# A decoder layer with a streamed cache: the pace of the stream, its rest before a pool switch, and norm factors in two parts

## The chip, the cores and the metric

The kernel runs on one core of a Trainium2 chip. The time is that of the device for one execution of the program, in microseconds (us), on that core. Lower is better. Engines are called as in the profile: PE (TensorE, matrix products), DVE (VectorE), ACT (ScalarE), POOL (GpSimd), SP (SyncE, which only issues DMAs).

## The reference

One step of a hybrid decoder layer for 512 prompt tokens and 32 sample tokens (8 sequences of 4), in float32. Cut to what matters here:

```python
z = rms_norm(x) @ w_in                      # (tokens, 2560): q, k, v, u, gv
q = rms_norm(q per head half of 64); k = rms_norm(k per head half of 64)
gv = rms_norm(gelu(gv) per group of 128); u = gelu(u)
att = softmax(q0 k0) v - lam * softmax(q1 k1) v        # prompt: causal, 512 tokens
att_s = the same for the 32 sample tokens, over 4096 cached keys and values
        of each of the 8 sequences (gathered by a page table) and the new ones
mix = u * (W_s gv + b)                      # within chunks of 128 positions
h   = x + [rms_norm(att), mix] @ w_out
out = h + relu(rms_norm(h) @ w_up)**2 @ w_down         # 1024 -> 4096 -> 1024
```

The cache holds 8 x 4096 rows of keys and as many of values, 512 floats each: 134 MB in all, which the kernel must read once.

## The kernel before

**The main program.** `in_proj` makes the input projection in ten pieces of 256 columns (q0 q1 k0 k1 v0 v1 g0 g1 u0 u1), each for four token tiles of 128 and the 32 sample rows; a piece's tiles come in two pairs (`tp` 0 and 1). Then come the prompt's attention (16 units), the output projection, and the feed-forward part (`ffn`) in eight groups of 512 hidden columns: in a group, an up product for each of the four tiles of 128 hidden columns (two passes `pr`, in each two tiles `f`, and each in two halves), then a down product with its own four parts. Float32 is made of a high and a low part, so a product is three matmuls: `wh` and `wl` are the parts of a weight tile `raw` (ACT casts the high part, DVE makes the low one), `Thi` and `Tlo` those of the tokens, `a_hi` and `a_lo` (both named `a`) those of the squared relu. `square` makes these: relu on ACT to `t`, the square on DVE, a cast on ACT, a difference on DVE. SP loads the weights, 512 KB each.

**The norm factors.** For q and k pieces `post` puts the sums of squares of each tile into a few columns of `ssb` (4 per tile, 2 in g pieces; DVE). When all tiles are there, `finish_piece` queues `stat`, which makes the factors of the whole piece on POOL with `rsqrt` (a short instruction that scales, then a long one that raises to the power -1/2), then `norm(i)` for each tile (DVE, or DVE and ACT, to `zn`) and `tr(i)` (PE transposes, `d<-idt,zn`). `later(fn, d)` queues a step and `flush`, called between pieces of the main program, runs what is due.

**The stream.** The cache of the 32 sample tokens is read in 64 chunks of 512 rows, 1 MB of keys and 1 MB of values each. POOL issues the gathers (`gK`, `gV`: DMA_INDIRECT to `kraw` and `v`; two `kraw`, four `v` buffers). For a chunk, `k_tr` transposes the keys on DVE to `kt` and then asks for the key load two chunks on; `scores` (PE, `S<-kt,qz`, two chunks at a time); after eight chunks (one sequence) `sm1` and `sm2` make the softmax (`s`, the matmul `d<-s,Rm`, the maximum `mc`, the exponentials `P` on ACT); `ptr` transposes on DVE and copies to `PT` on ACT (16 copies each); `av` multiplies with the values (PE, `O<-v,PT`) and then asks for the value load four chunks on; `fin1` scales (DVE `om`) and `fin2` sums with a matmul (`d<-om,selb`). The entries stand in the list `micro` in this order, each with a weight, 65.0 in all. Every `yield cost` of the main program goes to `pump`, which puts out as many entries as the credit pays for:

```python
    TAU = (122.7 + 44.8 * G1 + 30.0 * ATTW) / sum(w for w, _ in micro)   # G1 = 5, ATTW = 1.6
    def pump(dt):
        kv["t"] += dt
        while kv["i"] < len(micro) and kv["t"] >= micro[kv["i"]][0] * TAU:
            w, fs = micro[kv["i"]]
            kv["t"] -= w * TAU
            kv["i"] += 1
            for f, args in fs:
                f(*args)
```

The stream ends in feed-forward group 4 (`switch`), where the pools of the stream are closed ahead of the second pass:

```python
            if switch and pr == 1:
                while kv["i"] < len(micro):
                    pump(1.0)
                second_phase()
```

**The order.** A scheduler orders each engine's instructions. The wrapper `Ordered` (whose `call`, line 52, is the line of nearly all rows of the profile) binds it: POOL keeps the order of the program, PE and DVE may move an instruction past at most 28, and ACT's order is free. A tile's name says what is written, and what it is read from stands behind the arrow.

The functions that the diff touches and those that call them, with the line numbers of the profile:

Of the kernel before, what the change touches and what calls it, by code (L numbers as in the profile page):

```python
# [20 lines left out]
EPS = 1e-6  # L21
# [4 lines left out]
G1 = 5  # L26
# [9 lines left out]
ATTW = 1.6  # L36
# [26 lines left out]
def kernel(  # L63
# [230 lines left out]
    def later(fn, d=1):  # L294

        pend[d - 1].append(fn)
# [7 lines left out]
    def rsqrt(x, eps, mul=1.0):  # L304

        n, k = x.shape
        if eps or mul != 1.0:
            G.tensor_scalar(out=x, in0=x, scalar1=mul, scalar2=eps, op0=ALU.mult, op1=ALU.add)
        G.tensor_tensor(out=x, in0=x, in1=mhalf[:n, 0:k], op=ALU.pow)
# [74 lines left out]
    def pinned(on):  # L384

        for e in (V, A, PE, G, SP):
            e.window = 1 if on or e is G else WINDOW if e is V or e is PE else 0
# [282 lines left out]
    micro = []  # L670
# [26 lines left out]

    micro.append((0.2, [(lambda: sample_merge(), ())]))
    kv = {"i": 0, "t": 0.0, "on": False}
    TAU = (122.7 + 44.8 * G1 + 30.0 * ATTW) / sum(w for w, _ in micro)  # L700

    def pump(dt):

        if not kv["on"]:
            return
# [7 lines that stand above are left out]
# [45 lines left out]
        V.transpose(out=qT4[:, 8 * p:8 * p + 8, :], in_=zs[0:32].rearrange("p (f d) -> p f d", f=8))  # L758
        later(lambda: tr_pair(zs, 32, qTs[:, 2 * p:2 * p + 2, :], None), 2)

    def finish_piece(kind, p, ss, items):
        cols = slice(256 * p, 256 * p + 256)
        w = 4 if kind in "qk" else 2

        def stat():
            rsqrt(ss[:, 0:w * len(items)], EPS if kind in "qk" else 4.0 * EPS)

        def norm(i):
            z, n, t = items[i]
            sc = ss[:n, w * i:w * i + w]  # L770
            if kind == "g":
                gv_norm(z, n, sc, 2 * p)
                if t == 4:
                    SP.dma_start(out=gso[:, cols], in_=aux["gvs"][:, cols])
                return
            head_norm(z, n, sc, kg if kind == "k" else None)
            if kind == "k":
                SP.dma_start(out=kp[:, t, cols] if t < 4 else kso[:, cols], in_=z[:n])

        def tr(i):  # L780
            z, n, t = items[i]
            if kind == "g":
                return
            dst = (qT if kind == "q" else kT)[:, 2 * p:2 * p + 2, 128 * t:128 * t + 128] if t < 4 else \
                kTs[:, 2 * p:2 * p + 2, :]
            tr_pair(z, n, dst, qcol if kind == "q" else None)

        later(stat)
        for i in range(len(items)):
            later(lambda i=i: norm(i), 1 + i // 2)  # L790
            later(lambda i=i: tr(i), 3 + i // 2)

# [43 lines left out]
    def in_proj(gm, F, gsrc, junk):  # L836
        held = []
        pinned(True)
        zq = []

        def first_q(p):
            held.append((w_get(), w_get()))
            sps = dt_()[0:64, 0:256]
            for hf in range(2):
                packed(*held[p][hf], [(4 * hf + b, b) for b in range(4)], sps, hf == 0, hf == 1)
            return sps

        def first_stat(p, sps):
            z = combine(sps)
            zq.append(head_stat(z[0:32], 32, cst[0:32, 4 * p:4 * p + 4], 4))  # L850

        def first_keys():
            x_tile(2)
            k_tr(0)
            for p in range(2):
                q_sample(p, zq[p], cst[0:32, 4 * p:4 * p + 4])
            k_tr(1)
            kv["on"] = True

        sps = first_q(0)  # L860
        x_tile(0)
        w_conv()
        x_gain(gm, 1)
        x_stat(0, [xt[0]], 128, junk, G)
        x_gain(gm, 2)
        x_tile(1)
        x_gain(gm, 3)
        first_stat(0, sps)
        first_stat(1, first_q(1))
        rsqrt(cst[:32, 0:8], EPS)  # L870
        first_keys()
        yield 1.7
        att = attention()
        nt = new_tokens()
        for pi in range(10):
            kind, p = "qkvgu"[pi // 2], pi % 2
            if pi == 4:
                aux["vs"] = vgs
            if pi == 6:
                R3 = big.tile([128, 4 * T], F32, tag="r3", name="mix")  # L880
                R.append(R3)
                mix.append(R3[:, 0:2048].rearrange("p (n c) -> p n c", n=4))
                aux["gvs"] = vgs
            ss = ssb[pi % 2]
            items = []
            if kind == "q":
                A_, B_ = held[p]
            else:
                A_, B_ = w_get(), w_get()
            for tp in range(2):  # L890
                pss = {}
                if 2 * pi + tp == ATT0:
                    for _ in range(4):
                        flush()
                    local_pool(3)
                for half, w in ((0, A_), (1, B_)):
                    for t in (2 * tp, 2 * tp + 1):
                        cost = next(att, 0.0) if 2 * pi + tp >= ATT0 else 0.0
                        if half == 0:
                            pss[t] = dt_()[:, 0:256]  # L900
                        optB(pss[t], t, *w, half)
                        if t == 3 and (half == 0 or pi != 1):
                            w_conv()
                        if t % 2 == 1:
                            flush()
                        if half == 1:
                            post(kind, p, t, pss[t], 128, ss, items)
                            if pi == 4 and t == 0:
                                params()
                            if pi == 4 and t == 3:  # L910
                                params2()
                            if pi == 9 and t > 0:
                                cat_tile(t - 1)
                            if t == 3 and items:
                                finish_piece(kind, p, ss, items)
                            if pi == 0 and t == 1:
                                pinned(False)
                        elif pi == 5:
                            next(nt, None)
                        if pi == 0:  # L920
                            if t == 1 and half == 0:
                                x_stat(1, xt[1:4], 128, junk, G)
                                x_tile(3)
                            if t == 1 and half == 1:
                                masks(F, gsrc)
                            if t == 3 and half == 0:
                                gcols(gsrc)
                        if pi == 1 and t == 0 and half == 1:
                            load_params()
                        yield 1.3 + cost  # L930
                    if tp == 0 and kind != "q":
                        if half == 0:
                            sps = dt_()[0:64, 0:256]
                        packed(*w, [(4 * half + b, b) for b in range(4)], sps, half == 0, half == 1)
                        if half == 1:
                            post(kind, p, 4, combine(sps)[0:32], 32, ss, items)
                        yield 0.9
        yield from out_proj(att)

    def new_tokens():  # L940
# [212 lines left out]
    def ffn(start, joint, last, small, switch=False):  # L1153
        rng = [(0, 272), (272, 544)] if joint else [(0, 512)]
        n = T if joint else TP
# [14 lines left out]
        for pr in range(2):  # L1170
# [21 lines left out]
            for f in range(2):  # L1192
                if start and pr == 0:
                    square([psf[f]], f)
                    continue
                ps = [dt_() for _ in rng]
                for half in range(2):
                    hiw, low = hp[half]
                    for b in range(4):
                        k = 4 * half + b  # L1200
                        fc = slice(128 * f, 128 * f + 128)
                        for w, (st_w, mv) in enumerate(((hiw, Thi), (hiw, Tlo), (low, Thi))):
                            for q, (a, e) in enumerate(rng):
                                mm(ps[q][:, 0:e - a], st_w[:, b, fc], mv[:, k, a:e], k == 0 and w == 0, k == 7 and w == 2)
                    if f == 1:
                        w_conv()
                    if half == 0:
                        flush()
                        yield 2.8
                ff = 2 * pr + f  # L1210
                square(ps, ff)
                yield 2.8
# [237 lines left out]
```

## Time and profile before

| | |
|---|---|
| median of 3 runs | 822.18 us (821.0 to 822.18) |
| profiled execution | 821.3 us, of which the span from the first to the last instruction is 819.6 |
| mean granted clock of PE | 0.991 |
| busy: PE, weight loads, DVE, ACT, POOL | 97%, 77%, 66%, 44%, 22% |
| read from memory | 213.53 MB, 266 GB/s over the span |

Busy is the time in which an engine works on an instruction; the weight loads overlap PE's matmuls. In a row of a timeline, the time in brackets is the idle time ahead of the instruction, and behind the arrow stands what ended it.

### The profile page before, as it was taken

The numbers are of one execution on the slowest core, as the hardware profiler recorded it, in microseconds if no ns is written. First come the engines' busy times: TensorE is split into PE (matmuls) and PEld (weight loads), VectorE is DVE, ScalarE is ACT, GpSimd is POOL, SyncE is SP. The second block draws the span as 40 slices with busy tenths as digits, with TensorE's granted clock in tenths as the row PEclk, the third lists the DMA queues.
The fourth block names the chain that finished last, engine by engine and source line by source line (L and its number), as shares of the span: only waits on it lengthen the run. The fifth ranks groups of instructions, "written<-read, shape, count | busy, mean of one in ns | idle before, by whom it ended". The sixth has DMA issues, their size and how long they took to land.

```text
span 819.6 us, 15373 instructions
## 1 busy us (share of the span) xinstructions
PE 795.7 (97%) x6210; PEld 632.9 (77%) x6210; DVE 537.1 (66%) x883; ACT 358.6 (44%) x892; POOL 178.2 (22%) x196
## 2 busy tenths in 40 slices
PE   5899999999999999999999999998999999999997
PEld 4888887767667888867776777675676999998997
DVE  5878866898997856887677667653464534444254
ACT  4644743776585466463144235234243431331331
POOL 4553431344241222221322321213010000000000
PEclk9799999999999999999999999999999999999999
DMA  8597698787787888877997888877459677576202
GB/s 296 207 391 280 240 344 314 272 317 285 279 321 273 309 310 309 325 283 282 366 366 304 318 325 336 322 264 261 168 182 339 209 244 239 174 239 214 70 18 94
DMA packets 101798, 219.05 MB, mean 267 GB/s; under 512 B 6090, under 2 KB 83999, under 8 KB 85343
## 3 DMA queue, kind: packets, MB, share of 16 engines
q0 software_dynamic: 18432, 134.23, 42.4%
q1 hardware_dynamic: 83294, 83.84, 31.5%
q8 instruction: 49, 0.80, 0.4%
q14 instruction: 23, 0.18, 0.1%
HBM read 213.53 MB, written 4.52 MB: 266 GB/s over the span
## 4 chain that ended last, share of the span: by engine, by line
PE 73%; DVE 8%; issue 8%; ACT 4%; DMA 3%; POOL 2%; SPq 0%; DVEq 0%; POOLq 0%; ACTq 0%
PE d L52 64%; PE S L52 5%; PE O L52 5%; DVE kt L52 2%; ACT PT L52 2%; DMA kraw<-in_cache_k_dram,idxK 2%; DMA v<-in_cache_v_dram,idxK 1%; DMA raw<-in_w_in_dram 1%; ACT wh L52 1%; POOL v L52 1%; DVE zn L52 1%; DVE s L52 1%; POOL ssb L52 1%; DVE wl L52 1%; POOL kraw L52 1%
## 5 line engine op out<-in xcount | busy, mean ns | idle before, releaser
L52 ACT CAST wh<-raw 128x1024 fp32r<-128x1024 f32 x90 | 94.2, 1047 | 175.8 <-PE d L52 139.2
L52 PE MATMUL d<-a,wh 128*128 128x272 f32 (+1 forms) x704 | 168.3, 341 | 0.0
L52 DVE STREAM_TRANSPOSE kt<-kraw 128x2048 f32<-128x2048 f32 x64 | 146.3, 2297 | 16.6 <-PE S L52 7.4
L52 DVE TENSOR_TENSOR wl<-raw,wh 128x1024 fp32r<-128x1024 f32 x90 | 109.7, 1220 | 50.8 <-ACT wh L52 50.4
L52 PEld LDWEIGHTS d<-a,wh 128*128 128x128 f32 x704 | 113.2, 188 | 25.1 <-issue 6.3
L52 PE MATMUL d<-wh,Thi 128*128 128x256 f32 x432 | 127.7, 296 | 1.6 <-ACT t L52 1.6
L52 POOL DMA_INDIRECT v<-in_cache_v_dram,idxK x64 | 64.6, 1009 | 281.3 <-PE O L52 270.9
L52 PE MATMUL d<-wl,Thi 128*128 128x256 f32 x432 | 122.9, 285 | 0.0
L52 PE MATMUL d<-wh,Tlo 128*128 128x256 f32 x432 | 122.3, 284 | 0.0
L52 PE MATMUL d<-Thi,wh 128*128 128x272 f32 (+2 forms) x368 | 108.1, 334 | 0.0
L52 PE MATMUL d<-Tlo,wh 128*128 128x272 f32 (+2 forms) x368 | 106.5, 330 | 0.0
L52 PE MATMUL d<-Thi,wl 128*128 128x272 f32 (+2 forms) x368 | 106.4, 329 | 0.0
L52 PE MATMUL d<-a,wl 128*128 128x272 f32 (+1 forms) x352 | 104.2, 337 | 0.0
L52 PEld LDWEIGHTS d<-wh,Thi 128*128 128x128 f32 x432 | 82.3, 191 | 9.0 <-issue 4.8
L52 POOL DMA_INDIRECT kraw<-in_cache_k_dram,idxK x64 | 69.6, 1088 | 83.8 <-DVE kt L52 49.9
L52 PEld LDWEIGHTS d<-wh,Tlo 128*128 128x128 f32 x432 | 82.3, 191 | 0.4 <-issue 0.4
L52 PEld LDWEIGHTS d<-wl,Thi 128*128 128x128 f32 x432 | 82.1, 190 | 0.4 <-issue 0.4
L52 PEld LDWEIGHTS d<-Thi,wh 128*128 128x128 f32 x368 | 63.5, 188 | 15.6 <-issue 5.4
L52 ACT COPY PT<-d 32x128 f32<-32x128 f32 x256 | 65.6, 256 | 10.7 <-DVE d L52 7.5
L52 PEld LDWEIGHTS d<-Thi,wl 128*128 128x128 f32 x368 | 63.4, 188 | 6.2
L52 PEld LDWEIGHTS d<-Tlo,wh 128*128 128x128 f32 x368 | 63.7, 188 | 5.8
L52 PEld LDWEIGHTS d<-a,wl 128*128 128x128 f32 x352 | 60.5, 188 | 7.4 <-issue 0.4
(270 smaller groups left out, 1063.5 us busy)
## 6 DMA issues: line engine op xcount, KB each, us to landing
raw<-in_w_up_dram SPq DMA_DIRECT2D x32, 512.0 KB, 5.5
raw<-in_w_down_dram SPq DMA_DIRECT2D x32, 512.0 KB, 5.1
plain<-in_w_up_dram SPq DMA_DIRECT2D x20, 512.0 KB, 4.9
plain<-in_w_down_dram SPq DMA_DIRECT2D x20, 512.0 KB, 5.6
raw<-in_w_in_dram SPq DMA_DIRECT2D x18, 512.0 KB, 10.1
raw<-in_w_out_dram SPq DMA_DIRECT2D x8, 512.0 KB, 10.1
plain<-in_w_out_dram SPq DMA_DIRECT2D x8, 512.0 KB, 4.6
r<-in_x_prompt_dram SPq DMA_DIRECT2D x4, 512.0 KB, 9.0
```

The source lines that it names most:

```text
L52: r = f(*args, **kw)
```

## The change

Three edits. The constant of `TAU` falls from 122.7 to 117.7. In `ffn` of group 4, after the first half of the second up product of the first pass, the entries of the stream except the last five are put out. And the factors of a piece with norms are made in two parts: `early_stat` queues them for the first pair of tiles (and in k and g pieces the sample rows) when that pair is done, and `finish_piece` gets their number `n0`, makes the factors of the rest only, and queues this ahead of `norm(2)` and not ahead of `norm(0)`.

```diff
--- before.py
+++ after.py
@@ -697,7 +697,7 @@
 
     micro.append((0.2, [(lambda: sample_merge(), ())]))
     kv = {"i": 0, "t": 0.0, "on": False}
-    TAU = (122.7 + 44.8 * G1 + 30.0 * ATTW) / sum(w for w, _ in micro)
+    TAU = (117.7 + 44.8 * G1 + 30.0 * ATTW) / sum(w for w, _ in micro)
 
     def pump(dt):
 
@@ -758,12 +758,18 @@
         V.transpose(out=qT4[:, 8 * p:8 * p + 8, :], in_=zs[0:32].rearrange("p (f d) -> p f d", f=8))
         later(lambda: tr_pair(zs, 32, qTs[:, 2 * p:2 * p + 2, :], None), 2)
 
-    def finish_piece(kind, p, ss, items):
+    def early_stat(kind, ss, items):
+
+        n = (4 if kind in "qk" else 2) * len(items)
+        later(lambda: rsqrt(ss[:, 0:n], EPS if kind in "qk" else 4.0 * EPS))
+        return len(items)
+
+    def finish_piece(kind, p, ss, items, n0):
         cols = slice(256 * p, 256 * p + 256)
         w = 4 if kind in "qk" else 2
 
         def stat():
-            rsqrt(ss[:, 0:w * len(items)], EPS if kind in "qk" else 4.0 * EPS)
+            rsqrt(ss[:, w * n0:w * len(items)], EPS if kind in "qk" else 4.0 * EPS)
 
         def norm(i):
             z, n, t = items[i]
@@ -785,8 +791,9 @@
                 kTs[:, 2 * p:2 * p + 2, :]
             tr_pair(z, n, dst, qcol if kind == "q" else None)
 
-        later(stat)
         for i in range(len(items)):
+            if i == 2:
+                later(stat)
             later(lambda i=i: norm(i), 1 + i // 2)
             later(lambda i=i: tr(i), 3 + i // 2)
 
@@ -912,7 +919,7 @@
                             if pi == 9 and t > 0:
                                 cat_tile(t - 1)
                             if t == 3 and items:
-                                finish_piece(kind, p, ss, items)
+                                finish_piece(kind, p, ss, items, n0)
                             if pi == 0 and t == 1:
                                 pinned(False)
                         elif pi == 5:
@@ -935,6 +942,8 @@
                         if half == 1:
                             post(kind, p, 4, combine(sps)[0:32], 32, ss, items)
                         yield 0.9
+                if tp == 0 and items:
+                    n0 = early_stat(kind, ss, items)
         yield from out_proj(att)
 
     def new_tokens():
@@ -1207,6 +1216,9 @@
                     if half == 0:
                         flush()
                         yield 2.8
+                        if switch and pr == 0 and f == 1:
+                            while kv["i"] < len(micro) - 5:
+                                pump(1.0)
                 ff = 2 * pr + f
                 square(ps, ff)
                 yield 2.8
```

POOL has 208 rows instead of 196: six pairs more. On POOL, where the stream starts (loads of V and K, and the factors `ssb` of the pieces q0 and q1, here `ssb0` and `ssb1`), the program before has:

```order
L52 TENSOR_SCALAR rst8_119<-cst_117 128x3
L52 DMA v_442<-in_cache_v_dram,idxK_105 128x2048
L52 DMA v_516<-in_cache_v_dram,idxK_105 128x2048
L52 DMA kraw_583<-in_cache_k_dram,idxK_105 128x2048
L52 DMA v_598<-in_cache_v_dram,idxK_105 128x2048
L52 DMA kraw_601<-in_cache_k_dram,idxK_105 128x2048
L52 TENSOR_SCALAR ssb0_120<-ssb0_120 128x16
L52 TENSOR_TENSOR ssb0_120<-ssb0_120,mhalf_118 128x16
L52 DMA v_663<-in_cache_v_dram,idxK_105 128x2048
L52 DMA kraw_696<-in_cache_k_dram,idxK_105 128x2048
L52 DMA kraw_743<-in_cache_k_dram,idxK_105 128x2048
```

and the changed one:

```order
L52 TENSOR_SCALAR rst8_119<-cst_117 128x3
L52 DMA v_442<-in_cache_v_dram,idxK_105 128x2048
L52 TENSOR_SCALAR ssb0_120<-ssb0_120 128x8
L52 TENSOR_TENSOR ssb0_120<-ssb0_120,mhalf_118 128x8
L52 DMA v_518<-in_cache_v_dram,idxK_105 128x2048
L52 DMA kraw_562<-in_cache_k_dram,idxK_105 128x2048
L52 DMA v_600<-in_cache_v_dram,idxK_105 128x2048
L52 DMA kraw_603<-in_cache_k_dram,idxK_105 128x2048
L52 TENSOR_SCALAR ssb0_120<-ssb0_120 128x8
L52 TENSOR_TENSOR ssb0_120<-ssb0_120,mhalf_118 128x8
L52 DMA v_665<-in_cache_v_dram,idxK_105 128x2048
L52 DMA kraw_698<-in_cache_k_dram,idxK_105 128x2048
```

The loads are, in their order, V0, V1, K4, V2, K5, V3, K6 and K7 (values or keys of the chunk of that number; K0 to K3 were asked for before). The long pair of q0 (128x16, behind the second key load of the list) has become two pairs of 128x8, of which the first stands between the first and the second load of V.

On PE, the place in feed-forward group 4 where the last entries come out. `a0_4228` and `a1_4229` (`a0_4244`, `a1_4245` after) are the squared activations, `d` the sums of an up or a down product, `O` the products of sequence 6 and `om`, `selb` its `fin2`. Before, in the first down product:

```order
L52 MATMUL d_5963<-a1_4229,wh_5802 128x512 x2
L52 MATMUL d_5963<-a1_4229,wl_5803 128x512
L52 MATMUL O_5713<-v_5834,PT_5654 32x512 x4
L52 MATMUL O_5713<-v_5840,PT_5654 32x512 x4
L52 MATMUL d_6030<-om_6008,selb0_98 64x512
L52 MATMUL d_6032<-lm_5515,selb0_98 64x8
L52 MATMUL d_6047<-a0_4228,wh_5888 128x512 x2
```

`fin2` follows directly on the last `O` of its sequence. After, in the last up product of the first pass, and 20 rows further in the first down product:

```order
L52 MATMUL d_5920<-Thi_85,wl_5731 128x512
L52 MATMUL d_5939<-s_5903,Rm_95 128x4
L52 MATMUL O_5691<-v_5804,PT_5666 32x512 x4
L52 MATMUL O_5691<-v_5810,PT_5666 32x512 x4
L52 MATMUL d_5920<-Thi_85,wh_5825 128x512
L52 MATMUL d_5920<-Tlo_86,wh_5825 128x512
L52 MATMUL d_5920<-Thi_85,wl_5826 128x512
```

```order
L52 MATMUL d_6009<-a0_4244,wl_5846 128x512
L52 MATMUL d_6009<-a1_4245,wh_5845 128x512 x2
L52 MATMUL d_6009<-a1_4245,wl_5846 128x512
L52 MATMUL d_6042<-om_5963,selb0_98 64x512
L52 MATMUL d_6008<-a1_4245,wh_5845 128x512
L52 MATMUL d_6009<-a1_4245,wh_5845 128x512
L52 MATMUL d_6044<-lm_5470,selb0_98 64x8
```

`O` stands in the middle of the up product right behind `d<-s,Rm`, and the matmul with `om` comes behind the rest of the up product (12 matmuls) and 18 matmuls of the down product, ahead of the ones that read the last part of `a1`.

On ACT at the same place (`t` is the relu of an up product, `P` the exponentials, `PT` the copies). Before:

```order
L52 CAST wh_5888<-raw_5693 128x1024
L52 CAST wh_5939<-raw_5788 128x1024
L52 ACTIVATE t_5945<-d_5875 128x512
L52 ACTIVATE P_5955,mc_5952<-S_5554,mc_5952 128x512
L52 ACTIVATE P_5955,mc_5952<-S_5813,mc_5952 128x512
L52 CAST a1_4229<-t_5945 128x512
L52 COPY PT_6013<-d_6011 32x16x8 x13
L52 CAST wh_5988<-raw_5806 128x1024
L52 COPY PT_6013<-d_6011 32x16x8 x3
L52 COPY PT_6038<-d_6036 32x16x8 x16
```

In the changed program the same place reads:

```order
L52 CAST wh_5933<-raw_5734 128x1024
L52 ACTIVATE P_5944,mc_5941<-S_5532,mc_5941 128x512
L52 ACTIVATE P_5944,mc_5941<-S_5783,mc_5941 128x512
L52 COPY PT_5968<-d_5966 32x16x8 x16
L52 CAST wh_5997<-raw_5829 128x1024
L52 ACTIVATE t_6003<-d_5920 128x512
L52 COPY t_6244<-osum_130 64x512
L52 CAST a1_4245<-t_6003 128x512
L52 COPY PT_6050<-d_6048 32x16x8
L52 CAST wh_6034<-raw_5849 128x1024
```

The relu of the last up product of the pass (`t_5945` before, `t_6003` after) stood ahead of the exponentials and all copies; it stands behind them and 16 copies now.

## Rows read from the trace of the kernel before

**Rows 1.** The page's busy times by engine: us, share, instructions.
```profile
PE 795.7 (97%) x6210; PEld 632.9 (77%) x6210; DVE 537.1 (66%) x883; ACT 358.6 (44%) x892; POOL 178.2 (22%) x196
```

**Rows 2.** What TensorE waited for: total us, times, longest us.
```profile
PE O L52 <- DMA v<-in_cache_v_dram,idxK: 0.8, 1, 0.8
```

**Rows 3.** POOL timeline, 41 to 66 us: start, duration, instruction, idle before.
```profile
42.72 1.70 POOL L52 DMA_INDIRECT v<-in_cache_v_dram,idxK  x1 [0.30 <-issue]
...
48.92 1.65 POOL L52 DMA_INDIRECT kraw<-in_cache_k_dram,idxK  x1 [0.67 <-DVE kt L52]
...
50.94 2.94 POOL L52 TENSOR_TENSOR ssb<-ssb,mhalf 128x16 f32<-128x16 f32 x1
```

**Rows 4.** POOL by line, operation and shape.
```profile
L52 POOL TENSOR_TENSOR cst<-cst,mhalf 32x8 f32<-32x8 f32 x1 | 1.7, 1678 | 0.1
```

**Rows 5.** DVE timeline, 43 to 75 us.
```profile
45.73 0.70 DVE L52 TENSOR_REDUCE ssb<-z 128x4 f32<-128x256 f32 x2
...
54.80 2.31 DVE L52 STREAM_TRANSPOSE kt<-kraw 128x2048 f32<-128x2048 f32 x1 [0.26 <-DMA kraw<-in_cache_k_dram,idxK]
...
61.63 2.31 DVE L52 STREAM_TRANSPOSE kt<-kraw 128x2048 f32<-128x2048 f32 x1 [0.79 <-DMA kraw<-in_cache_k_dram,idxK]
```

**Rows 6.** Busy time in a stretch, the last three: PEclk, DMA share, GB/s.
```profile
45.00:50.00 5.00, 5.00 (x45) 5.00 (x44) 5.00 (x6) 2.44 (x5) 2.95 (x3) 1.00 0.98 368
```

**Rows 7.** The key tiles `kraw` from 40 to 76 us, issue to landing.
```profile
DMA to landing us min/median/max: 5.6/8.0/12.7
```

**Rows 8.** SyncE's queue, 40 to 80 us.
```profile
43.61 33.26 SPq L52 DMA_DIRECT2D raw<-in_w_in_dram  x4
```

**Rows 9.** TensorE timeline, 32 to 68 us.
```profile
36.27 0.30 PE L52 MATMUL d<-idt,zn 32*128 32x32 f32 x2 [1.93 <-ACT z L52]
...
64.00 1.93 PE L52 MATMUL S<-kt,qz 128*32 128x256 f32 x32 [0.51 <-DVE kt L52]
```

**Rows 10.** Busy time in two stretches: PE, PEld, DVE, ACT, POOL.
```profile
150.00:200.00 50.00, 49.26 (x424) 35.30 (x423) 44.91 (x94) 39.52 (x129) 17.94 (x18) 1.00 0.78 282
200.00:250.00 50.00, 47.33 (x392) 32.60 (x392) 44.03 (x91) 32.48 (x101) 16.17 (x17) 1.00 0.84 317
```

**Rows 11.** TensorE timeline, 546 to 577 us.
```profile
547.28 0.40 PE L52 MATMUL d<-Thi,wl 128*128 128x512 f32 x1
547.51 0.28 PE L52 MATMUL d<-s,Rm 128*128 128x4 f32 x2
...
557.43 1.07 PE L52 MATMUL d<-om,selb 128*64 128x512 f32 x2 [2.12 <-DVE om L52]
...
564.25 3.64 PE L52 MATMUL O<-v,PT 128*32 128x512 f32 x32
```

**Rows 12.** ACT timeline, 545 to 575 us.
```profile
548.47 0.59 ACT L52 ACTIVATE t<-d 128x512 f32<-128x512 f32 x1
548.96 0.68 ACT L52 ACTIVATE P<-S,mc 128x512 f32<-128x512 f32 x1
...
550.46 0.62 ACT L52 CAST a<-t 128x512 fp32r<-128x512 f32 x1
551.10 3.47 ACT L52 COPY PT<-d 32x128 f32<-32x128 f32 x13
554.47 1.04 ACT L52 CAST wh<-raw 128x1024 fp32r<-128x1024 f32 x1
```

**Rows 13.** DVE timeline, 545 to 575 us.
```profile
547.83 0.16 DVE L52 TENSOR_REDUCE mc<-d 128x1 f32<-128x4 f32 x1 [3.38 <-PE d L52]
...
549.74 0.68 DVE L52 TENSOR_TENSOR t<-t 128x512 f32<-128x512 f32 x1
...
555.54 1.22 DVE L52 TENSOR_TENSOR wl<-raw,wh 128x1024 fp32r<-128x1024 f32 x1 [1.37 <-ACT wh L52]
```

**Rows 14.** Busy time in two stretches, PEclk the third from the end.
```profile
37.00:40.50 3.50, 3.50 (x20) 3.50 (x19) 2.97 (x6) 1.91 (x4) 1.97 (x4) 0.51 0.71 285
557.00:560.50 3.50, 3.07 (x13) 2.12 (x14) 1.76 (x4) 2.30 (x10) 0.58 (x1) 1.00 0.96 339
```


## The prediction

> **What bounds the kernel now.** I read the busy shares of the page first, then the waits of TensorE (PE), then its timeline round each wait. PE works for 795.7 us, 97% of the span [rows 1]: a microsecond of any other engine counts only where PE stands still for it, so the change is worth what it does to PE's few gaps. Behind the set-up these are short and single: 0.51 us for the transposed key tile `kt` at 64.00 [rows 9], 2.12 us for DVE's `om` at 557.43 [rows 11], 0.8 us for one load of V [rows 2], and some in the prompt's attention from 150 to 250 us, where PE is busy 49.26 and 47.33 of 50 us while DVE is at 44.91 and 44.03 [rows 10]. When the cached stream is started, the DMA engines and not PE are full: from 45 to 50 us they are busy at a share of 0.98 and move 368 GB/s [rows 6]. So three places decide: the start of the stream, the attention, and the stream's last entries.
>
> **The early factors (first place).** POOL works in the order of the program, and the order now has the first new pair of instructions, for piece q0, between the first two loads of V. The pair needs the sums of squares of token tiles 0 and 1, which DVE makes in 0.70 us from 45.73 [rows 5]: they are there at 46.4. A pair with 128x8 has no row. The same eight columns on 32 partitions took 1.68 us [rows 4], 128x16 took 2.94 [rows 3]; I take 1.7, by the equal columns, and 0.3 for the short instruction ahead of it (what lies between the end of the load at 48.92 and the long one at 50.94 [rows 3]). So POOL is free at 48.4. V1, which was issued at 42.72 [rows 3], comes 5.7 us later, and behind it in POOL's queue K4, V2 and K5.
>
> How much of these 5.7 us reaches K5 depends on what the loads waited for. K5 was issued at 48.92 [rows 3], and DVE waited for its data until 61.63 [rows 5]: 12.7 us, the longest landing of that stretch, where the shortest is 5.6 [rows 7]. It stood behind other loads. K4's data were there at 54.80 [rows 5], so V2 and K5 took 6.83 us, 3.4 each. Counted back by 3.4, V1 was there at 51.4 and V0 at 48.0. Of the 5.6 us of the shortest landing, 3.4 are the transfer and 2.2 the lead from the issue to the first byte. In the changed kernel V1's bytes then begin at 48.4 + 2.2 = 50.6 instead of 48.0: the queue of cached loads runs dry for 2.6 us. The next loads are issued faster (some 1.7 us for each at most [rows 3]) than they move, so nothing is added behind V1. A part comes back, because weights move faster in the dry time: SyncE issues four loads of 512 KB in 33.26 us [rows 8], and what is left of one of them at that moment, a quarter of a MB at most, is worth up to 0.7 us of the engines' time; I take 0.4. K5 is there 2.2 us later.
>
> Its transpose and the scores of chunks 4 and 5 follow. PE waited 0.51 us for them at 64.00 [rows 9]; in the new order they stand three matmuls later, 0.34 us (three of half the columns of those that take 0.23, below). PE waits 2.2 − 0.3 = **+1.9 us** more, and nothing gives it back, since PE hardly waits again for what lies behind. Bounds: 0 (K5 in time after all) and +2.9 (K5's issue moves from 48.92 to 48.4 and three loads of 1.2 us, 3.2 us, and PE sees all of it but the 0.3).
>
> The Trainium skill has a rule against this term: "DMA: Bandwidth & Descriptors", section "Queues, rings and completion order", says that each DMA engine takes turns, packet by packet, between all queues for which it has work, so that what one queue leaves is used by another. With enough weights waiting the term would be near 0 by that. The rate of rows 8, 2 MB in 33 us beside 368 GB/s, says that too few are waiting here.
>
> The five other new pairs cost POOL 1 to 2 us each, in idle time: POOL's gaps of this stretch are waits for DVE. Two waits of DVE for these factors vanish later; PE didn't wait behind them, so they count 0.
>
> **The earlier stream (second place).** A unit of weight in the stream's list is now due every 389.7/65 = 5.995 units of the main program's cost instead of every 394.7/65 = 6.072: 1.3% sooner, and 5 units (about microseconds) at the end. In the attention that decides which collisions happen: PE's gaps there are 0.74 + 2.67 = 3.4 us [rows 10], and DVE at 90% leaves little to hide a new one. I take 0, between −2 and +2. From 250 us to the last entries PE has no wait that a shift could remove.
>
> **The last entries (third place).** `d<-om,selb` of sequence 6 stood right behind the last product O of its group; in the new order it stands behind the second half of the last up product of the first pass and most of the first down product, 12 and 18 matmuls of 0.23 us (547.28 to 547.51 [rows 11]), 6.9 us. Its wait of 2.12 us goes: **−2.1**. The products O of the group come sooner, so POOL may ask for V61 sooner, for which PE waited 0.8 us [rows 2]: **−0.7** (0 to −0.8).
>
> The price stands on ACT: the relu of the last up product stood ahead of the two exponentials and the copies to `PT`; now it stands behind both exponentials, 16 copies and one cast. Counted from the matmul `d<-s,Rm` (547.51 [rows 11]): DVE's maximum begins at +0.3 [rows 13] and with two short instructions the exponentials can begin at +0.7. From the first exponential to the first copy are 2.14 us (548.96 to 551.10 [rows 12]), to +2.8; 16 copies take 16/13 of 3.47, 4.3, to +7.1; the cast 1.04, to +8.2; the relu 0.59, to +8.8. On DVE the low part of the weights, 1.22, stands ahead of the square, 0.68 [rows 13]: from +8.2 to +9.4 and +10.1. The cast of its high part takes 0.62 [rows 12], to +10.7. PE comes to the matmul that needs it at 0.1 + 0.9 (a quarter of the 32 products O in 3.64) + 6.9 + 0.5 (`om`) [rows 11] = +8.5. It waits about **+2.1**: bounds 0 (a product O or a load of V that holds PE up in between) and +2.5. This place: −2.1 − 0.7 + 2.1 = −0.7 (−2.9 to +0.4).
>
> **The loop for the rest.** It puts out entries until five are left; where it stands all are out already, by the count of the entries and of the units of weight up to there. The order has the same rows with and without it: 0.
>
> **Sum.** +1.9 + 0 − 0.7 = +1.2 on the profiled execution's 821.3 us (the span of 819.6 and 1.7 around it): 822.5. The median of the runs, 822.18, lies 0.9 above the profiled execution, so **823.4 us**. 0.2% is 1.64 us, about what a measurement of this kernel can tell from no change; the forecast lies inside it, on the slow side.
>
> **Rivals.**
> *Slower: the clock falls behind the new gap.* The wait at 64 us becomes 0.5 + 1.9 = 2.4 us. Behind the 1.93 us wait at 36.27 [rows 9] the granted clock was 0.51 from 37 to 40.5 us [rows 14], the lower level of 1.2 GHz: 3.5 us at half speed, 1.7 lost. Behind the 2.12 us before 557.43 it stayed at 1.00 [rows 14]. If it falls: 823.4 + 1.7 = 825.1. It decides once the new gap is of the first one's length, 1.9 us; one of the two gaps of that length speaks for it and one against.
> *The loads hide the first place.* Weights fill the dry time, or K5 is in time: +1.9 becomes 0, 821.5, no change.
> *Faster: the attention's gaps close.* They are single collisions, and the stream moves against them; all 3.4 us gone gives 820.0. Against it: the same shift makes new ones, with DVE at 90%.
> *The relu is in time.* The 2.1 us don't come: 821.3, no change.
>
> **Chances.** My forecast 0.44 (0.24 within 0.2%, 0.17 slower, 0.03 faster, by its terms' bounds); the clock 0.18, slower; hidden loads 0.16 (0.12 within, 0.04 faster); the attention 0.12, faster; the relu 0.10 (0.07 within, 0.03 faster). Together faster 0.22, same 0.43, slower 0.35. The range, 819.6 to 826.2, holds the four rivals and goes past the clock's by the first place's upper bound (2.9 − 1.9); the forecast's own is 821.0 to 825.0.
>
> **What would show it.** V1 issued near 48.4 instead of 42.72; K5's transpose near 63.8 instead of 61.63; PE waiting some 2.4 us for `kt` near 66; no wait for `om` in the last entries; a wait of about 2 us for the squared activations in the first down product after them. Wrong: K5's transpose at its old time (hidden loads); a granted clock of half behind 66 us (the clock); PE busy over 98 of the 100 us of the attention; a down product that doesn't wait (the relu). The whole is wrong if PE gets gaps of over 2 us where it has none now, above all in the feed-forward groups between 250 us and the last entries.

## The result and the profile after

The changed kernel takes 827.63 us (median of 6 runs, 826.76 to 831.23); the kernel before took 821.89 beside it. The ratio is 1.0081 (95% interval 1.0068 to 1.0094): **slower by 0.8%**, some 6 us, where 823.4 was forecast and 826.2 was the upper end. The range was missed.

The profiled execution of the changed kernel took 829.32 us with a span of 827.5, so it stands 1.7 above its median; the span of before is 819.6. To see where the 7.9 us between the spans arise, I took a matmul of the main program (all but the stream's `S`, `O`, `om`, `lm` and `s`) by its number, which is the same in both traces, and subtracted the starts, and what the stream had put in between the two. At the 180th matmul it is 42.64 against 41.18, at the 620th 114.69 against 110.46, at the 1500th 270.70 against 265.07, at the 3000th 632.70 against 624.83. In stretches (named by the time before):

| stretch | forecast | after less before, us |
|---|---|---|
| up to 41 us (the same instructions in both) | 0 | +1.5 |
| 41 to 76, the stream's start | +1.9 | +2.4 |
| 76 to 110, pieces k and v | 0 | +0.4 |
| 110 to 265, the attention | 0 | +1.4 |
| 265 to 527 | 0 | +0.3 |
| 527 to 625, the last entries | -0.7 | +2.0 |
| behind that | 0 | +0.1 |

The first row is no effect of the change: in the profiled executions of the twelve kernels below, which have the same instructions up to there, it lies between -1.1 and +1.5. In both profiles the granted clock is at its full level from 42 us to the last microsecond, so no row behind the first holds a fall of the clock.

**The stream's start** went as the prediction said, with one more wait of PE ahead of the one that it priced. POOL's timeline (start, duration, instruction, idle time ahead and its releaser), to be held against [rows 3]:

```profile
47.66 0.19 POOL L52 TENSOR_SCALAR ssb<-ssb 128x8 f32<-128x8 f32 x1 [3.81 <-DVE ssb L52]
47.94 1.68 POOL L52 TENSOR_TENSOR ssb<-ssb,mhalf 128x8 f32<-128x8 f32 x1
49.81 1.07 POOL L52 DMA_INDIRECT v<-in_cache_v_dram,idxK  x1 [0.19 <-issue]
...
53.67 0.94 POOL L52 DMA_INDIRECT kraw<-in_cache_k_dram,idxK  x1 [0.30 <-issue]
```

The long instruction of the pair takes 1.68 us (1.7 was taken), and V1 is issued at 49.81, 48.35 without the 1.46 us of the first stretch (48.4 was forecast). The DMA engines run dry. The stretch from 50 to 55 us, first before, then in the changed kernel (the last two columns are their share and GB/s; from 45 to 50 us the share was 0.98 before and is 0.82 now):

```profile
50.00:55.00 5.00, 5.00 (x59) 3.94 (x58) 1.82 (x5) 1.68 (x4) 4.65 (x4) 1.00 1.03 425
```
```profile
50.00:55.00 5.00, 5.00 (x61) 4.11 (x59) 3.05 (x7) 1.68 (x4) 3.93 (x6) 1.00 0.67 231
```

So the weights did not fill the gap. They used it as long as there were some: the share is 0.99 from 48 to 49 us, 0.39 in the next microsecond and 0.01 from 50 to 51, and SyncE issues its next load at 51.24. The Trainium skill's rule that was weighed there ("DMA: Bandwidth & Descriptors", "Queues, rings and completion order") agrees with this; what was missing is work in the other queue. DVE's timeline, against [rows 5]:

```profile
59.92 2.31 DVE L52 STREAM_TRANSPOSE kt<-kraw 128x2048 f32<-128x2048 f32 x1 [3.92 <-DMA kraw<-in_cache_k_dram,idxK]
62.16 1.18 DVE L52 TENSOR_TENSOR wl<-raw,wh 128x1024 fp32r<-128x1024 f32 x1
63.26 0.75 DVE L52 TENSOR_TENSOR zn<-zn,ssb 128x256 f32<-128x256 f32 x2
63.93 0.41 DVE L52 TENSOR_REDUCE ssb<-z 128x4 f32<-128x256 f32 x1
65.57 2.31 DVE L52 STREAM_TRANSPOSE kt<-kraw 128x2048 f32<-128x2048 f32 x1 [1.23 <-DMA kraw<-in_cache_k_dram,idxK]
```

K5 is transposed at 64.1 without the 1.46 (63.8 was forecast). PE is held up sooner, by K4, which the prediction didn't follow: DVE stood 3.92 us for that load, and the second norms of q0 (`zn`) are queued behind its transpose. PE's timeline, against [rows 9]:

```profile
63.82 0.75 PE L52 MATMUL d<-idt,zn 128*128 128x128 f32 x4 [2.23 <-DVE zn L52]
...
67.94 1.93 PE L52 MATMUL S<-kt,qz 128*32 128x256 f32 x32 [0.60 <-DVE kt L52]
```

Behind the 2.23 us for the norms PE still waits 0.60 us for K5's `kt`. So by these rows `S` could not have begun before 67.94 without the wait for the norms either: K5 sets the delay, as forecast (67.94 less 1.46 is 2.5 us behind the 64.00 of before), and the wait for K4 lies inside it.

**The last entries** went the other way. PE's timeline, against [rows 11] and [rows 2]:

```profile
559.72 1.07 PE L52 MATMUL d<-om,selb 128*64 128x512 f32 x2
562.06 0.73 PE L52 MATMUL d<-a,wh 128*128 128x512 f32 x2 [1.26 <-ACT a L52]
...
580.27 1.93 PE L52 MATMUL O<-v,PT 128*32 128x512 f32 x16
583.03 1.06 PE L52 MATMUL O<-v,PT 128*32 128x512 f32 x8 [0.84 <-DMA v<-in_cache_v_dram,idxK]
585.99 1.07 PE L52 MATMUL O<-v,PT 128*32 128x512 f32 x8 [1.89 <-DMA v<-in_cache_v_dram,idxK]
```

The wait for `om` is gone and that for `a` is there, as forecast. The wait for V61 is gone too, but V62 and V63 now cost 0.84 and 1.89. **The attention** lost 1.1 us of PE's busy time from 150 to 250 us, against [rows 10] (PE is the first column after the length):

```profile
150.00:200.00 50.00, 48.04 (x414) 34.84 (x412) 41.54 (x96) 35.08 (x119) 17.82 (x19) 1.00 0.72 274
200.00:250.00 50.00, 47.49 (x400) 33.14 (x401) 46.78 (x92) 35.38 (x110) 17.50 (x19) 1.00 0.80 306
```

### The profile page after: what moved, and what is told of

Its sections match the earlier page's. It is cut to its first block, busy times and chain, and to the rows that moved or that the text cites. A ratio compares the mean times of both kernels' runs of the same rounds, so it can differ in the third digit from the quotient of the medians.

```text
span 827.5 us, 15381 instructions
## 1 busy us (share of the span) xinstructions
PE 798.1 (96%) x6210; PEld 632.7 (76%) x6210; DVE 537.5 (65%) x883; ACT 358.5 (43%) x892; POOL 183.7 (22%) x208
## 4 chain that ended last, share of the span: by engine, by line
PE 69%; issue 9%; ACT 8%; DVE 6%; DMA 5%; POOL 2%; SPq 0%; DVEq 0%; POOLq 0%; ACTq 0%
PE d L52 61%; PE S L52 4%; PE O L52 4%; DMA kraw<-in_cache_k_dram,idxK 3%; ACT PT L52 3%; DVE kt L52 2%; ACT z L52 2%; POOL v L52 1%; DMA v<-in_cache_v_dram,idxK 1%; ACT t L52 1%; DMA raw<-in_w_in_dram 1%; DVE wl L52 1%; ACT wh L52 1%; POOL kraw L52 1%; ACT P L52 0%
## 5 line engine op out<-in xcount | busy, mean ns | idle before, releaser
L52 PE MATMUL O<-v,PT 128*32 128x512 f32 x512 | 63.4, 593 | 2.7 <-DMA v<-in_cache_v_dram,idxK 2.7
```

The costliest lines, as they stand in the source:

```text
L52: r = f(*args, **kw)
```

## The experiments

Theory A: the change is a sum of separate effects, those of the factors in two parts and those of the pace, each in a stretch of its own. Its rivals differ from run to run and stand in the expectations. Times are medians; the ratio is to the kernel before on the same chip, and a difference given as +x or -x us is this ratio's share of 822 us. Theory A's numbers were worked out anew from the traces at hand as the runs went on. The loop for the rest got no run: without it each engine has the same instructions in the same order.

**stat_only: the factors alone.** The changed kernel with two edits taken back:

```diff
-    TAU = (117.7 + 44.8 * G1 + 30.0 * ATTW) / sum(w for w, _ in micro)
+    TAU = (122.7 + 44.8 * G1 + 30.0 * ATTW) / sum(w for w, _ in micro)
-                        if switch and pr == 0 and f == 1:
-                            while kv["i"] < len(micro) - 5:
-                                pump(1.0)
```

> The factors in two parts alone, at the old pace of the stream and without the loop. Theory A (three places add up: the start of the stream loses about 2.4 us through the early pair of q0 on POOL, the pace of the stream loses about 1.5 us in the attention and 2.0 us in the last entries): +2.5 us, between +1.5 and +3.5, a wait of PE of about 2 us near 61 us, and the last entries as before with the wait of 2.1 us for om. Rival B (the pace is the cause of nearly all): within 1 us of before.

Measured: 822.64 us, ratio 0.9999 (0.9987 to 1.0010). The wait at the start is there, and so is its loss, +2.1 from 41 to 76 us:

```profile
63.26 0.74 PE L52 MATMUL d<-idt,zn 128*128 128x128 f32 x4 [1.79 <-DVE zn L52]
```

But -1.5 from 76 to 110 and -1.2 in the attention give it back. By the total rival B was right; by the stretches the start costs what theory A says, and the factors have gains that I had counted as nothing.

**tau_only: the pace alone.** The kernel before with the constant 117.7.

> The pace of the stream alone (constant 117.7). Theory A: +3.5 us (attention +1.5, last entries +2.0), the start as before with key load 5 transposed near 61.6 us. Rival B: +5 to +6 us. Rival C (the shift of the stream costs only together with the late start): within 1 us of before.

Measured: 829.63 us, ratio 1.0091 (1.0071 to 1.0111), +7.5. That is above theory A's +3.5 and above rival B's +5 to +6: the pace alone costs as much as the whole change, and rival C falls. In the profiled execution it is +1.9 from 76 to 110 us, where theory A had nothing, +2.5 in the attention and +1.2 in the last entries.

**q0_whole: the changed kernel with q0's factors in one part.**

```diff
-                    n0 = early_stat(kind, ss, items)
+                    n0 = early_stat(kind, ss, items) if pi else 0
-            if i == 2:
+            if i == (2 if n0 else 0):
                 later(stat)
```

> The changed kernel, but the factors of piece q0 made in one part, so that no factor stands between the first two loads of V. Theory A: 2.4 us less than the changed kernel, about 825.2 us, with the second load of V issued at about 42.7 and no wait of 2 us near 61 us. Rival D (the delay comes from the stream's pace or from other early pairs): as the changed kernel, 827.6 us.

Measured: 826.87 us, ratio 1.0047 (1.0030 to 1.0064); the changed kernel has 1.0081, so 0.34% or 2.8 us less, as theory A says; from 41 to 76 us -0.2 in place of +2.4. Rival D falls.

**rest_split: old pace, no loop, q0 in one part** (the diffs of stat_only and q0_whole together).

> Old pace, no loop, the factors in two parts in every piece but q0. Theory A (the parts of the change add up: the split of q0 loses 2.0 to 2.4 us at the start, the splits of the later pieces give back 1.2 us near 97 us and 1.2 us in the attention): 2 us less than before, about 820.5 us. Rival E (what was given back after 97 us was only the late start made up, not a gain of its own): within 0.7 us of before.

Measured: 818.40 us, ratio 0.9964 (0.9950 to 0.9977): **3.0 us faster than before**. Theory A holds and rival E falls: the splits of the later pieces are a gain of their own, -1.4 from 76 to 110 and -1.2 in the attention.

**att_early, early97, att_only: the pace by stretch.** `repace` changes the pace and gives the credit that the new pace would have given up to there:

```diff
+    def repace(c):
+        nonlocal TAU
+        done = sum(w for w, _ in micro[:kv["i"]])
+        kv["t"] += TAU * done
+        TAU = (c + 44.8 * G1 + 30.0 * ATTW) / sum(w for w, _ in micro)
+        kv["t"] -= TAU * done
...
+            if pi == 5:
+                repace(122.7)
```

This is early97 (constant 117.7 at first). att_only has 122.7 at first, `repace(117.7)` in that place and `repace(122.7)` ahead of feed-forward group 0; att_early has 117.7 at first and only the latter.

> The kernel before with the new pace up to the end of the output projection and the old pace, with its old credit, from feed-forward group 0 on. Theory A: +4.5 us, between 3 and 6: the waits near 97 us and in the attention cost that, the last entries nothing. Rival F (the loss of the pace alone is mostly that of the last entries and of falls of the clock behind their waits): +1 to +2 us.

> The new pace only until the sixth piece of the input projection, the old pace and credit from there on, so that nothing differs from before behind about 110 us. Theory A: a wait of PE of about 2 us near 96 us for ACT z, since the transpose of a key chunk on DVE now stands ahead of a 0.3 us instruction on the sample rows for which ACT waits; +1.3 us, and up to +2 with the fall of the clock behind it in some executions. Rival F: 0.

> The old pace until the sixth piece, the new one from there to the end of the output projection, the old one in the feed-forward groups. Theory A: +2.7 us, between 1.7 and 3.7, in the attention alone, so that this and early97 add up to att_early's +4.6. Rival F: below +1 us.

Measured: att_early 825.78 us, 1.0056 (1.0042 to 1.0069), +4.6; early97 824.54, 1.0029 (1.0019 to 1.0039), +2.4; att_only 825.34, 1.0035 (1.0023 to 1.0047), +2.9. The two parts make 0.64% against 0.56% together, and rival F falls in all three; early97 lies above theory A's +2. early97 differs from before on PE in only three places, and shows the mechanism best. The timelines of DVE, ACT and PE in early97:

```profile
94.66 0.40 DVE L52 TENSOR_TENSOR zn<-d,zn 32x256 f32<-32x256 f32 x1
94.99 2.29 DVE L52 STREAM_TRANSPOSE kt<-kraw 128x2048 f32<-128x2048 f32 x1
97.21 0.30 DVE L52 TENSOR_SCALAR zn<-zn,cst 32x256 f32<-32x256 f32 x1
```
```profile
97.55 0.40 ACT L52 COPY zn<-zn 32x256 f32<-32x256 f32 x1 [2.74 <-DVE zn L52]
97.86 0.41 ACT L52 ACTIVATE z<-zn 32x256 f32<-32x256 f32 x1
98.17 0.45 ACT L52 ACTIVATE zn<-d,cst 128x256 f32<-128x256 f32 x1
98.53 0.45 ACT L52 ACTIVATE z<-d,rst 128x256 f32<-128x256 f32 x1
```
```profile
99.03 0.38 PE L52 MATMUL d<-wh,Thi 128*128 128x256 f32 x1 [2.10 <-ACT z L52]
```

In before the two stand the other way round on DVE:

```profile
94.42 0.56 DVE L52 TENSOR_SCALAR zn<-zn,cst 32x256 f32<-32x256 f32 x1
...
95.24 2.29 DVE L52 STREAM_TRANSPOSE kt<-kraw 128x2048 f32<-128x2048 f32 x1
```

In early97 a key transpose of 2.29 us has got ahead of a 0.30 us instruction on the sample rows. ACT works in the order that it was given and stands 2.74 us for that one, until 97.55; behind it are the reads of sums `d`, and PE waits 2.10 us for ACT. In before and in rest_split the same instruction comes ahead of this transpose. ACT waits for it there too, 1.14 us in rest_split and 2.81 in before (behind the transpose at 91.24, one sooner), but goes on at 94.26 and 95.08, and PE's wait near 97 us is none and 0.48. So it is not the length of ACT's wait that costs, but that ACT comes 2.5 us later to what PE needs (first the row of rest_split, then that of before):

```profile
94.26 0.42 ACT L52 ACTIVATE z<-zn 32x256 f32<-32x256 f32 x1 [1.14 <-DVE zn L52]
```
```profile
95.08 0.42 ACT L52 ACTIVATE z<-zn 32x256 f32<-32x256 f32 x1 [2.81 <-DVE zn L52]
```

The wait is one part of the cost. From the main program's matmul at 95.1 us of before to that at 106.0 the profile of early97 takes 2.5 us more, counted from start to start: PE's waits are 1.6 us longer, the main matmuls take 1.5 us more (the clock has fallen, last section), and the products `S` take 0.6 us less, since 32 of them stand in one row, in before in three rows of 4, 26 and 2. In rest_split, which has the one row too, the same stretch is 1.4 us shorter than before: 0.5 by the wait, 0.6 by `S` and 0.3 by the other matmuls.

In the attention PE has the same kinds of waits at the new pace, more of them: five waits for `t` in att_only (3.0 us), three in the changed kernel (2.7), two before (2.2). Which instruction each of these stands behind I have not taken apart.

**tau_120: half the change of the pace** (constant 120.2).

> Half the change of the pace alone (constant 120.2). Rival G (an earlier stream costs in proportion): +3 to +4 us. Theory A (the pace moves single collisions, each of which is there or not): no proportion, anything from -2 to +7 us, and waits of PE in other places than at 117.7.

Measured: 822.76 us, ratio 1.0010 (0.9999 to 1.0021). Rival G falls: half the shift doesn't cost half. That is a balance and not the absence of effects: in the profile its attention is 1.2 us shorter than before (at 117.7 it is 2.5 longer), and the stretch from 41 to 76 us is 1.7 longer.

**end_early: the pace from feed-forward group 2 on.** The kernel before with this ahead of each group's `ffn` (the lines of `repace` written out):

```diff
+        if g == 2:
+            repace(117.7)
```

> The kernel before until feed-forward group 2, where the stream gets the new pace and the credit that the new pace would have given up to there, so that the last entries come out as in the changed kernel. Theory A: +2.0 us, all of it in the last entries (a wait for a of 1.3 us and waits for the loads V61 and V63 of 2.7 us, no wait for om). By the prediction's third place: -0.7 us. Rival C: 0.

Measured: 824.45 us, ratio 1.0016 (1.0000 to 1.0031), +1.3. The sign is theory A's, the size between its +2.0 and nothing; the prediction's -0.7 falls. The loads that PE waits for are V62 and V63 (0.74 and 1.87 us), not V61 and V63 as I had written. The runs spread from 821.2 to 827.1; the last section has a likely reason.

**end_kraw: end_early with V62 and V63 asked for at once.**

```diff
-            t = kvp.tile([128, 2048], F32, tag="v", name="v", bufs=VB)
+            t = kvp.tile([128, 2048], F32, tag="kraw", name="v", bufs=KB) if n >= NCH - 2 else \
+                kvp.tile([128, 2048], F32, tag="v", name="v", bufs=VB)
...
-        gV(n + VB)
+        if n + VB < NCH - 2:
+            gV(n + VB)
+        if n == NCH - 7:
+            gV(NCH - 2)
+            gV(NCH - 1)
```

> end_early with the last two loads of values put into the two key buffers, which are free by then, and asked for right behind the load of chunk 61, so that they don't wait for a buffer of values. Theory A (in the early last entries PE waits for the load of chunk 63 because its buffer comes free late): 1.9 us less than end_early, so -0.6 to 0 us against before, no wait near 578 us and no fall of the clock behind it. Rival H (the load is late because the DMA engines are full): no change against end_early, +1.3 us.

Measured: 820.82 us, ratio 0.9982 (0.9971 to 0.9994): 1.5 us faster than before, 2.8 less than end_early. POOL in end_early (V60 to V63) and then in end_kraw (V61 to V63):

```profile
560.57 1.69 POOL L52 DMA_INDIRECT v<-in_cache_v_dram,idxK  x1 [11.53 <-PE O L52]
562.57 0.94 POOL L52 DMA_INDIRECT v<-in_cache_v_dram,idxK  x1 [0.30 <-issue]
568.24 1.66 POOL L52 DMA_INDIRECT v<-in_cache_v_dram,idxK  x1 [4.73 <-PE O L52]
570.20 0.94 POOL L52 DMA_INDIRECT v<-in_cache_v_dram,idxK  x1 [0.30 <-issue]
```
```profile
564.67 0.94 POOL L52 DMA_INDIRECT v<-in_cache_v_dram,idxK  x1 [0.30 <-issue]
565.91 0.94 POOL L52 DMA_INDIRECT v<-in_cache_v_dram,idxK  x1 [0.31 <-issue]
567.16 0.94 POOL L52 DMA_INDIRECT v<-in_cache_v_dram,idxK  x1 [0.30 <-issue]
```

The 4.73 us in which POOL waited for `O` to free a buffer are gone, and PE does its last four chunks in one row without a wait. Rival H falls.

```profile
576.58 3.64 PE L52 MATMUL O<-v,PT 128*32 128x512 f32 x32
```

**rest_kraw and best: the parts that pay, together.** rest_kraw is rest_split with the diff of end_kraw; best has the pace from group 2 on as well.

> rest_split with the last two loads of values in the key buffers, at the old pace. Theory A (the parts add up): at the old pace the load of chunk 61 costs 0.5 to 0.9 us and the wait for om of 2.1 us stays, so at most 1 us less than rest_split: -3 to -4 us against before. Rival: the key buffers change nothing at the old pace, -3.0 us.

> rest_split, the last two loads of values in the key buffers, and the new pace from feed-forward group 2 on. Theory A: the 3.0 us of rest_split and the 1.5 us of end_kraw add up: -4.5 us against before, about 817.6 us, with neither the wait for om nor those for V61 and V63, and a wait for a of 1.25 us. Rival (the gains overlap, or falls of the clock move to other waits): -3 us.

Measured: rest_kraw 819.56 us, 0.9963 (0.9949 to 0.9977): no more than rest_split, so the rival holds and the key buffers pay only with the early last entries. best 816.78 us, 0.9932 (0.9918 to 0.9946): **5.6 us faster than before**, where the sum gives 4.5, at the edge of the interval, and faster than both kernels of this study. What PE waits for in best, behind the set-up:

```profile
PE d L52 <- ACT PT L52: 1.4, 2, 1.2
PE d L52 <- ACT a L52: 1.2, 1, 1.2
PE d L52 <- ACT t L52: 0.5, 2, 0.4
```

## Why the prediction was wrong, point by point

- **The early factors, q0: right.** +1.9 was forecast, +2.4 came in the changed kernel and +2.1 alone, and 2.8 us go when q0 is made whole again. V1's and K5's times were right to 0.3 us. I had not followed K4, for whose transpose PE stands 2.23 us; that this adds nothing is luck, since PE would have stood as long for K5's `kt` behind it.
- **The other early pairs, counted as 0: wrong.** "PE didn't wait behind them": they bring 1.4 to 1.5 us near 97 us and 1.2 us in the attention (rest_split, -3.0). I looked at the waits of DVE for the factors and not at ACT, which stands in order behind DVE's small instructions: the wait of 0.48 us for ACT goes, and 0.6 us come from the products `S` that stand in one row, which no wait shows. In the attention the wait of 1.56 us for `t` at 219 us in before is gone in rest_split; why, I have not taken apart. So the factors as a whole cost nothing (0.9999).
- **The earlier stream, 0 between -2 and +2: the step that failed.** It was weighed for the attention alone, as collisions that come and go at no cost on balance. It costs 2.9 us there (att_only, interval 1.9 to 3.9), beyond the bound; and 2.4 us near 97 us (early97), where I had no term at all. 0.29% and 0.35% of it and 0.16% in the last entries make 0.80%; the pace alone measured 0.91% (0.71 to 1.11), and the whole change, with the factors at nothing, 0.81%. In the changed kernel this loss and the gains of the other pairs fall into the same stretches, and its table shows only what is left of it: +0.4, where PE has no wait above 0.49 us near 97 us and so not the collision of early97, and +1.4. By that table the last entries are furthest off.
- **The last entries, -0.7 with a bound of +0.4: wrong, +1.3 to +2.0.** -2.1 for `om` and the end of the wait for V61 came. The wait for `a` was 1.26 us, not 2.1: the order's eight products O for two chunks are sixteen in the profile, so they take 1.9 us and not a quarter of 3.64. With the longer `om` too, PE comes to `a` 10.3 us behind the start of `d<-s,Rm` and not 8.5, and `a` is there at 11.6 and not 10.7. The sum failed by a wait that it didn't have: the last four chunks stand together now, and the loads of V62 and V63 can only be asked for when V58 and V59 are used (end_kraw).
- **The loop: right,** it does nothing.
- **The rivals.** The clock did not fall behind the new gap at 61 us, in the changed kernel or in stat_only, so the slower rival as it was put did not happen; it fell elsewhere (below). The attention moved, but to the other side than its rival. The loads did not hide the first place. Of the signs that were named, V1's and K5's times, the end of the wait for `om` and the wait for `a` all came: the sum was wrong in places for which it had no sign.

## What to carry to other kernels

A stream that is mixed into a full engine's work by a pace had no slope here: a shift of 1.3% moved a long transpose ahead of a short instruction, the one such meeting that was taken apart held PE for 2.10 us, and half the shift cost next to nothing in all. So price a shift by the queues that take their work in order (here ACT behind DVE's 0.3 us instruction, POOL's loads behind a factor), and test it by giving the shift to one stretch at a time. And when a tail is drawn together, ask when the buffers of its last loads come free.

## What the runs showed of the clock

A wait of PE of about 2 us cost more than itself in many of these executions. In early97 the granted clock (the third number from the end) was below 1.00 behind the 2.10 us wait:

```profile
98.00:101.00 3.00, 1.97 (x11) 1.97 (x12) 3.00 (x7) 3.00 (x9) 1.54 (x1) 0.75 0.72 255
101.00:104.00 3.00, 3.00 (x21) 2.80 (x24) 1.03 (x2) 2.87 (x13) 1.79 (x2) 0.68 1.06 397
104.00:107.00 3.00, 3.00 (x48) 1.30 (x40) 0.98 (x3) 1.51 (x6) 2.07 (x2) 1.00 0.69 248
```

In end_early it was 0.50, the lower level of 1.2 GHz, behind the waits for V62 and V63:

```profile
580.00:584.00 4.00, 3.94 (x13) 1.89 (x14) 0.69 (x1) 0.00 (x0) 0.00 (x0) 0.50 0.02 8
```

It is not the same in every execution. Behind the wait of 2.1 us for `om`, which is the same in seven profiled kernels, it fell in five (stat_only, rest_split, att_early, early97, att_only) and stayed at 1.00 in two (before, rest_kraw); where it fell the stretch from 527 to 625 us was 1.2 to 1.6 us longer, where not, -0.1 to 0. It fell in all three profiles with the wait near 97 us, and behind the waits for V in two of four (end_early, q0_whole; not in the changed kernel or tau_only). The length of the wait alone does not decide it: behind the 2.23 us of the changed kernel at 61 us it stayed at 1.00, and in tau_120 it was 0.57 from 602 to 606 us, where the only wait of the 15 us before is one of 0.75 us. In end_kraw it fell to 0.66 from 220 to 225 us, behind a wait of 1.56 us in the attention that before has as well. Where best has no wait above 1.25 us behind the set-up, its five runs lie within 0.8 us of each other (816.42 to 817.19), the twelve of end_early within 5.9. That the falls explain the whole spread I have not shown: each run but the profiled one has a time alone.
